# Partition sums of the modulation vectors: one DVE reduction over four transposed tiles in place of four accumulating ACTIVATEs

## The chip, the cores and the metric

The kernel runs on one core of a Trainium2 chip. The time is the device time of one execution in microseconds, taken as the median of several executions. The engines are PE (matrix products, with PEld for its weight loads), ACT (ScalarE), DVE (VectorE), POOL (GpSimd) and SP, whose queue issues most of the DMAs.

## What is computed

Two models run in one launch. The first is two stacked transformer layers over 256 tokens of width 1024. Each layer makes six modulation vectors from a conditioning vector and uses them to shift, scale and gate:

```
mod = jax.nn.silu(c) @ w_ada + b_ada
sh1, sc1, gt1, sh2, sc2, gt2 = jnp.split(mod, 6, axis=-1)
h = adaln(rms_norm(x, g_mix), sh1, sc1)        # h * (1 + scale) + shift
proj = h @ w_in                                # q, k, v and gates of two attentions
x = x + gt1[:, None, :] * (mixed @ w_out)
h = adaln(rms_norm(x, g_mlp), sh2, sc2)
u = jnp.square(jax.nn.relu(h @ w_up))
x = x + gt2[:, None, :] * (u @ w_down)
```

The second model is a layer with a pooling mixer and sixteen experts, then a layer with attention and sixteen experts; both take modulation vectors made in the same way from the same kind of product. Everything is in fp32.

## The kernel before

A vector of 1024 modulation values is a 1 x 1024 by 1024 x 1024 product. `ada_piece` (L335) does it without PE's main stream: the 1024 x 1024 block of the weight matrix comes in eight row pieces of 128 x 1024, and each piece is scaled by its 128 values of silu(c), one to a partition, and added to an accumulator `aacc` of 128 x 1024, by ACT for the first piece (L344) and by DVE for the seven others (L347). When the eighth piece is in (q == 7), the 128 partitions of `aacc` have to be summed. For 24 of the vectors this is done in two halves of four 128 x 128 blocks: PE transposes four blocks (L355) into a PSUM tile `tr`, of which there is one buffer, and four ACTIVATEs with `accum_out` (L358) sum one block each along its free side into a column of `u`. Each such ACTIVATE is followed by an instruction that reads the accumulator out. DVE then adds the bias (L367) and the vector `mod[m, v, j]` is there. The other vectors go through eight products with a vector of ones (L363).

Around this runs the main stream. All weights come as fp32 through SP's queue into seven `raw` buffers. `pump` (L297) splits a piece on chip into a high part `H` (ACT, L303) and a low part `L` (DVE, L304), of which five buffers each exist, and PE multiplies in three passes, high by high (L149), low weights (L150), low activations (L151). Modulation pieces come in the same list between the weight pieces, so `pump` serves both.

The norms ahead of the projections, `norm_1` and `norm_T_`, work on two tiles of 128 tokens: ACT sums squares (L542), POOL makes the reciprocal root, DVE scales the rows (L544), PE transposes them (L558), ACT (L573) and DVE (L571) apply shift and scale to alternate blocks, ACT casts the high part (L575) and DVE subtracts for the low part (L576). `residual_` multiplies a projection by its gate (L898) and adds it to x (L899); the gate's row is made from its `mod` vector by PE (L381) and ACT (L382). `mod_rows` (L986, L990, L991) is the norm of the second model's first layer.

Nothing here is ordered by hand. A tile scheduler takes the program with its dependencies and its priorities and writes one fixed list for each engine; every engine works its list strictly in order and waits on semaphores. `pump` gives modulation pieces a priority below the main stream's (offset -150), norms and residuals one above it (HP).

## Time and profile before

| | us |
|---|---|
| median of 3 runs | 1456.69 (1452.02 to 1458.51) |
| profiled execution | 1451.84 |
| its span | 1450.0 |
| PE busy | 1312.8 |
| DVE busy | 1184.0 |
| ACT busy | 904.9 |
| POOL busy | 192.9 |

The profile is of one execution, 4.85 us below the median of the runs. The modulation vectors that the change touches are summed between 96.8 and 823.0 us of its span. Stretches are named by the us from the start of the span; the first model runs to about 885 us, its second layer from about 435. A timeline row shows one instruction, or several alike in a row, with the idle time of its engine ahead of it and what ended that.

### The profile page before, as it was taken

The page shows a single profiled execution, that of the slowest core. Times are in us where ns is not written, and L with a number is a line of the kernel's source. Part 1 is how long each engine was busy: PE and PEld are TensorE (multiplying, and loading weights), DVE is VectorE, ACT ScalarE, POOL GpSimd, SP SyncE. Part 2 cuts the span into 40 slices and gives each one's busy share as a digit, 9 for nine tenths or more (in the row PEclk, how much of TensorE's full clock was granted, in tenths as well). Part 3 has the DMA queues.
Part 4 walks back from the last instruction along what each step waited for, and adds up shares of the span by engine and source line. Part 5 has one row for each costly group of instructions (what it writes and reads, how often), then busy time and mean ns, then how long its engine had stood idle before and what let it go on. Part 6 is the DMA issues. An engine that isn't in the chain of part 4 may idle for free. (4 is left out here: it accounts for less than half of the span.)

```text
span 1450.0 us, 20231 instructions
## 1 busy us (share of the span) xinstructions
PE 1312.8 (91%) x6943; PEld 1036.2 (71%) x6943; DVE 1184.0 (82%) x1719; ACT 904.9 (62%) x1726; POOL 192.9 (13%) x183
## 2 busy tenths in 40 slices
PE   3889999999998899988999998699998879989897
PEld 2666777898987667767899887577665756766575
DVE  6886697867778988898999888599888798598696
ACT  2476845665656678566765544399784558567584
POOL 0340011000002300121000022322211220110000
PEclk9998998999999999997999999699999999989899
DMA  9676686799784667886888987699986534259781
GB/s 368 199 250 199 231 295 218 274 305 317 266 305 132 217 190 251 267 252 226 298 318 282 338 297 233 204 349 327 324 305 223 165 110 145 89 193 375 290 310 53
DMA packets 109363, 362.16 MB, mean 250 GB/s; under 512 B 17998, under 2 KB 21558, under 8 KB 109248
## 3 DMA queue, kind: packets, MB, share of 16 engines
q1 hardware_dynamic: 105456, 351.26, 70.1%
q0 software_dynamic: 3360, 7.91, 2.3%
q10 hardware_dynamic: 432, 1.57, 0.3%
q8 instruction: 58, 0.95, 0.3%
q14 instruction: 57, 0.47, 0.1%
HBM read 351.70 MB, written 12.88 MB: 251 GB/s over the span
## 5 line engine op out<-in xcount | busy, mean ns | idle before, releaser
L303 ACT CAST H<-raw 128x1024 fp32r<-128x1024 f32 x331 | 345.7, 1049 | 227.3 <-PE acc L151 89.2
L304 DVE TENSOR_TENSOR L<-raw,H 128x1024 fp32r<-128x1024 f32 x331 | 410.0, 1247 | 70.0 <-ACT H L303 67.0
L347 DVE SCALAR_TENSOR_TENSOR page<-raw,sc,page 128x1024 f32<-128x1024 f32 x218 | 279.9, 1293 | 20.5 <-DMA raw<-in_w_ada_dram 11.8
L149 PE MATMUL mm<-H,page 128*128 128x512 f32 (+1 forms) x416 | 168.3, 407 | 15.3 <-ACT page L575 10.5
L150 PE MATMUL mm<-L,page 128*128 128x512 f32 (+1 forms) x416 | 166.1, 400 | 0.1
L151 PE MATMUL mm<-H,page 128*128 128x512 f32 (+1 forms) x416 | 165.4, 399 | 0.9 <-DVE page L576 0.8
L304 DVE TENSOR_TENSOR L<-page,H 128x1024 fp32r<-128x1024 f32 x104 | 125.3, 1222 | 29.5 <-ACT H L303 27.8
L149 PE MATMUL acc<-H,page 128*128 128x512 f32 x352 | 138.5, 394 | 0.0
L151 PE MATMUL acc<-H,page 128*128 128x512 f32 x352 | 138.5, 393 | 0.0
L150 PE MATMUL acc<-L,page 128*128 128x512 f32 x352 | 138.3, 393 | 0.0
L303 ACT CAST H<-page 128x1024 fp32r<-128x1024 f32 x104 | 108.3, 1053 | 40.2 <-PE mm L151 25.2
L800 PE MATMUL mm<-page,H 128*128 128x256 f32 x448 | 127.7, 286 | 0.0
L803 PE MATMUL mm<-page,L 128*128 128x256 f32 x448 | 127.6, 285 | 0.0
L802 PE MATMUL mm<-page,H 128*128 128x256 f32 x448 | 127.3, 284 | 0.0
L149 PE MATMUL mm<-H,gH 128*96 128x512 f32 x256 | 105.7, 413 | 8.9 <-PEq L1231 6.5
L149 PEld LDWEIGHTS mm<-H,page 128*128 128x128 f32 x416 | 81.5, 196 | 36.2 <-ACT page L575 12.9
L151 PE MATMUL mm<-H,gL 128*96 128x512 f32 x256 | 103.9, 406 | 1.3 <-DVE gL L1405 1.3
L150 PE MATMUL mm<-L,gH 128*96 128x512 f32 x256 | 103.0, 402 | 0.0
L151 PEld LDWEIGHTS mm<-H,page 128*128 128x128 f32 x416 | 81.4, 196 | 19.2 <-DVE page L576 3.3
L150 PEld LDWEIGHTS mm<-L,page 128*128 128x128 f32 x416 | 81.8, 197 | 16.2 <-issue 1.7
L800 PEld LDWEIGHTS mm<-page,H 128*128 128x128 f32 x448 | 86.1, 192 | 0.8
L802 PEld LDWEIGHTS mm<-page,H 128*128 128x128 f32 x448 | 85.8, 192 | 0.5
(377 smaller groups left out, 2530.2 us busy)
## 6 DMA issues: line engine op xcount, KB each, us to landing
raw<-in_w_mod_dram SPq DMA_DIRECT2D x94, 512.0 KB, 4.5
raw<-in_w_ada_dram SPq DMA_DIRECT2D x92, 512.0 KB, 5.1
raw<-in_w_in_dram SPq DMA_DIRECT2D x68, 512.0 KB, 4.4
raw<-in_moe_gu_dram SPq DMA_DIRECT2D x64, 512.0 KB, 6.3
raw<-in_w_up_dram SPq DMA_DIRECT2D x61, 512.0 KB, 5.3
raw<-in_w_down_dram SPq DMA_DIRECT2D x61, 512.0 KB, 5.0
page<-in_moe_gu_dram SPq DMA_DIRECT2D x61, 512.0 KB, 8.0
page<-in_moe_wd_dram SPq DMA_DIRECT2D x36, 512.0 KB, 11.0
```

Source lines behind the costliest of these rows:

```text
L149: mm(ps, sH, wH, start=start, stop=False)
L150: mm(ps, sH, wL, start=False, stop=False)
L151: mm(ps, sL, wH, start=False, stop=stop)
L303: s.nc.scalar.copy(H, src)
L304: s.nc.vector.tensor_sub(Lo, src, H.bitcast(F32))
L347: nc.vector.scalar_tensor_tensor(a, raw, c, a, ALU.mult, ALU.add)
L800: nc.tensor.matmul(o, a, H[q // 2][:, 2 * (q % 2) + k], start=q == 0 and k == 0 and f % 2 == 0, stop=False, skip_group_check=True)
L802: nc.tensor.matmul(o, a, Lo[q // 2][:, 2 * (q % 2) + k], start=False, stop=False, skip_group_check=True)
L803: nc.tensor.matmul(o, b, H[q // 2][:, 2 * (q % 2) + k], start=False, stop=q == 3 and k == 1 and f % 2 == 1, skip_group_check=True)
```

## The change

The four ACTIVATEs of a half become one DVE `tensor_reduce`, which sums along the innermost side of the tile seen as 128 x 4 x 128 and writes the four columns of `u` at once. The transposes ahead of it and the addition of the bias behind it stay.

```diff
--- before.py
+++ after.py
@@ -353,9 +353,7 @@
                         t = s.tr()
                         for i in range(4):
                             nc.tensor.transpose(t[:, i * P:(i + 1) * P], s.aacc[v][:, (4 * h + i) * P:(4 * h + i + 1) * P], s.ident)
-                        for i in range(4):
-                            o = t[:, i * P:(i + 1) * P]
-                            nc.scalar.activation(o, o, AF.Copy, accum_out=u[:, 4 * h + i:4 * h + i + 1])
+                        nc.vector.tensor_reduce(u[:, 4 * h:4 * h + 4], t.rearrange("p (a b) -> p a b", b=P), AX.X, ALU.add)
                     t = u
                 else:
                     t = s.mm() if m == 0 and j < 2 else s.tr()
```

192 ACTIVATEs and 192 accumulator reads leave ACT's list, 48 reductions enter DVE's. Since the scheduler places everything by its own reckoning, other instructions move as well. Lines behind 358 have a number lower by 2 in the changed kernel: L558 is L556 there, L576 is L574, L381 is L379.

The second norm of the first layer, on PE: `mm_2069` and `mm_2045` are the end of the out projection, `mm_2235` and `mm_2211` the start of the up projection, and `acc_2179` and `acc_2184` the second tile of tokens. Before:

```order
L151 MATMUL mm_2069<-H_2083,page_1919 128x512
L355 MATMUL tr_2004<-cst,page_1735 128x128 x4
L355 MATMUL tr_2013<-cst,page_1735 128x128 x4
L149 MATMUL mm_2235<-H_2089,page_2159 128x512
L150 MATMUL mm_2235<-L_2090,page_2159 128x512
L151 MATMUL mm_2235<-H_2089,page_2161 128x512
```

After, the same place, where the first group of transposes still stands:

```order
L151 MATMUL mm_2045<-H_2059,page_1901 128x512
L355 MATMUL tr_1986<-cst,page_1717 128x128 x4
L149 MATMUL mm_2211<-H_2065,page_2135 128x512
L150 MATMUL mm_2211<-L_2066,page_2135 128x512
L151 MATMUL mm_2211<-H_2065,page_2137 128x512
```

and further down, around the second group:

```order
L556 MATMUL acc_2179<-cst,page_2172 128x128 x4
L556 MATMUL acc_2184<-cst,page_2172 128x128 x4
L150 MATMUL mm_2211<-L_2217,page_2136 128x512
L151 MATMUL mm_2211<-H_2216,page_2138 128x512
L149 MATMUL mm_2211<-H_2225,page_2136 128x512
L150 MATMUL mm_2211<-L_2226,page_2136 128x512
L151 MATMUL mm_2211<-H_2225,page_2138 128x512
L149 MATMUL mm_2211<-H_2225,page_2136 128x512
L150 MATMUL mm_2211<-L_2226,page_2136 128x512
L151 MATMUL mm_2211<-H_2225,page_2138 128x512
L355 MATMUL tr_1992<-cst,page_1717 128x128 x4
```

The second group of transposes has moved from right behind the first to behind the transposes of the second tile of tokens (L556) and eight more products.

The second norm of the second layer, on DVE, from the scaled rows (L544, now L542) to the low part of the first tile's second half (L576, now L574). Before:

```order
L304 TENSOR_TENSOR L_6253<-raw_6084,H_6252 128x1024
L571 TENSOR_SCALAR q_1375_6189<-acc_6179,acol_6170,mod_3469 128x128
L571 TENSOR_SCALAR q_1376_6196<-acc_6184,acol_6170,mod_3469 128x128
L304 TENSOR_TENSOR L_6263<-raw_6096,H_6262 128x1024
L571 TENSOR_SCALAR q_1375_6189<-acc_6179,acol_6170,mod_3469 128x128
L571 TENSOR_SCALAR q_1376_6196<-acc_6184,acol_6170,mod_3469 128x128
L367 TENSOR_TENSOR mod_6019<-acol_1330_6000,cols 128x8
L347 SCALAR_TENSOR_TENSOR page_6071<-raw_6042,sc,page_6071 128x1024
L576 TENSOR_TENSOR page_6168<-q_1375_6189,page_6166 128x4x128
L347 SCALAR_TENSOR_TENSOR page_6070<-raw_6074,sc,page_6070 128x1024
L576 TENSOR_TENSOR page_6169<-q_1376_6196,page_6167 128x4x128
```

After:

```order
L304 TENSOR_TENSOR L_6139<-raw_5972,H_6138 128x1024
L304 TENSOR_TENSOR L_6145<-raw_5976,H_6144 128x1024
L569 TENSOR_SCALAR q_1375_6081<-acc_6071,acol_6062,mod_3421 128x128
L569 TENSOR_SCALAR q_1376_6088<-acc_6076,acol_6062,mod_3421 128x128
L356 TENSOR_REDUCE acol_1330_5904<-tr_5905 128x4
L569 TENSOR_SCALAR q_1375_6081<-acc_6071,acol_6062,mod_3421 128x128
L347 SCALAR_TENSOR_TENSOR page_5962<-raw_5864,sc,page_5962 128x1024
L574 TENSOR_TENSOR page_6060<-q_1375_6081,page_6058 128x4x128
L569 TENSOR_SCALAR q_1376_6088<-acc_6076,acol_6062,mod_3421 128x128
L304 TENSOR_TENSOR L_6155<-raw_5988,H_6154 128x1024
L574 TENSOR_TENSOR page_6061<-q_1376_6088,page_6059 128x4x128
```

Both L304 now stand ahead of the four blocks to which shift and scale are applied (L569), and the first reduction stands among these. The second one and the bias come right behind this stretch.

The end of the first model, on PE: `acc_61..` (`acc_62..` before) is the last down projection, `mm_8281` and `mm_8287` (`mm_8425` and `mm_8431` before) the row of the gate by which its result is multiplied. Before:

```order
L151 MATMUL acc_6235<-H_8468,page_8098 128x512
L149 MATMUL acc_6235<-H_8468,page_8097 128x512
L1092 MATMUL mm_8329<-Mt_8324,Q_1788_8322 96x32 x4
L381 MATMUL mm_8425<-cst,mod_4078 128x128 x4
L381 MATMUL mm_8431<-cst,mod_4078 128x128 x4
L150 MATMUL acc_6235<-L_8469,page_8097 128x512
L381 MATMUL mm_8440<-cst,acol_8437 128x128 x4
L381 MATMUL mm_8446<-cst,acol_8437 128x128 x4
L381 MATMUL mm_8453<-cst,mod_4630 128x128 x4
L381 MATMUL mm_8459<-cst,mod_4630 128x128 x4
L151 MATMUL acc_6235<-H_8468,page_8098 128x512
```

After:

```order
L151 MATMUL acc_6129<-H_8330,page_7954 128x512
L149 MATMUL acc_6129<-H_8330,page_7953 128x512
L150 MATMUL acc_6129<-L_8331,page_7953 128x512
L151 MATMUL acc_6129<-H_8330,page_7954 128x512
L1090 MATMUL mm_8185<-Mt_8180,Q_1788_8178 96x32 x4
L379 MATMUL mm_8281<-cst,mod_4018 128x128 x4
L379 MATMUL mm_8287<-cst,mod_4018 128x128 x4
L379 MATMUL mm_8296<-cst,acol_8293 128x128 x4
L379 MATMUL mm_8302<-cst,acol_8293 128x128 x4
L379 MATMUL mm_8309<-cst,mod_4564 128x128 x4
L379 MATMUL mm_8315<-cst,mod_4564 128x128 x4
```

The small product L1090 (L1092) and three pairs of L379 (L381), each pair one row spread over 128 partitions, stood among the last down projection's products, 31 of which came behind them; now all of them stand behind the last one.

ACT there, from the last two copies of those rows to the sum of squares of the second tile (L986, now L984). Before:

```order
L382 COPY page_8452<-mm_8453 128x512
L382 COPY page_8452<-mm_8459 128x512
L344 ACTIVATE page_8497<-raw_8404,sc 128x1024
L303 CAST H_8513<-raw_8478 128x1024
L986 ACTIVATE hrow_8583,ss_8584<-x 128x1024
L303 CAST H_11949<-raw_8481 128x1024
L303 CAST H_11961<-raw_8495 128x1024
L303 CAST H_11973<-raw_8499 128x1024
L382 COPY page_8607<-mm_8608 128x512
L382 COPY page_8607<-mm_8614 128x512
L382 COPY page_8620<-mm_8621 128x512
L986 ACTIVATE hrow_8593,ss_8594<-x 128x1024
```

After:

```order
L380 COPY page_8308<-mm_8309 128x512
L380 COPY page_8308<-mm_8315 128x512
L303 CAST H_8369<-raw_8334 128x1024
L984 ACTIVATE hrow_8439,ss_8440<-x 128x1024
L344 ACTIVATE page_8353<-raw_8260,sc 128x1024
L303 CAST H_11805<-raw_8337 128x1024
L984 ACTIVATE hrow_8449,ss_8450<-x 128x1024
```

The two sums of squares have come together: the first stands two instructions behind the copies, the second three further on.

## Rows read from the trace of the kernel before

**Rows 1.** The page, part 1: busy us (share of the span) x instructions of each engine.

```profile
PE 1312.8 (91%) x6943; PEld 1036.2 (71%) x6943; DVE 1184.0 (82%) x1719; ACT 904.9 (62%) x1726; POOL 192.9 (13%) x183
```

**Rows 2.** Everything of line 358; duration ns min/median/max, then who waited for it.

```profile
L358 ACT ACTIVATE tr<-tr x192: 251/262/298, 96.8 to 822.8; 128x128 f32<-128x128 f32 x192
L358 ACT ACTIVATION_READ_ACCUMULATOR tr<-tr x192: 180/194/214, 97.0 to 823.0; 128x1 f32 x192
...
  PE tr L355: 5.7, 6
```

**Rows 3.** DVE grouped by line and form: busy us, mean ns of one, idle before it.

```profile
L1589 DVE TENSOR_REDUCE mx<-acc 128x1 f32<-128x512 f32 x32 | 21.5, 684 | 1.2 <-PE acc L1587 1.0
...
L923 DVE TENSOR_REDUCE mx<-acc 128x1 f32<-128x256 f32 x32 | 13.3, 414 | 0.0
...
L922 DVE TENSOR_REDUCE mx<-acc 128x1 f32<-128x128 f32 x32 | 9.1, 285 | 9.7 <-PE acc L919 9.7
```

**Rows 4.** Waits of PE, 80 to 830 us: us in total, times, longest.

```profile
PE mm L149 <- ACT page L575: 8.1, 5, 2.9
...
PE tr L355 <- ACT tr L358: 5.7, 6, 2.5
```

**Rows 5.** Timeline of PE, 244 to 249: start, us, what [idle before <-releaser].

```profile
247.14 0.66 PE L355 MATMUL tr<-cst,page 128*128 128x128 f32 x4 [2.45 <-ACT tr L358]
...
248.72 0.58 PE L151 MATMUL mm<-H,page 128*128 128x512 f32 x1
```

**Rows 6.** Timeline of DVE, same stretch.

```profile
246.77 1.22 DVE L304 TENSOR_TENSOR L<-raw,H 128x1024 fp32r<-128x1024 f32 x1
247.98 0.69 DVE L576 TENSOR_TENSOR page<-q,page 128x512 fp32r<-128x512 f32 x1
```

**Rows 7.** Timeline of PE, first and second norm of the second layer, 450 to 657.

```profile
450.93 1.10 PE L558 MATMUL acc<-cst,page 128*128 128x128 f32 x8 [0.73 <-DVE page L544]
...
652.79 1.12 PE L355 MATMUL tr<-cst,page 128*128 128x128 f32 x4 [0.83 <-ACT tr L358]
655.85 1.12 PE L355 MATMUL tr<-cst,page 128*128 128x128 f32 x4 [1.94 <-ACT tr L358]
```

**Rows 8.** Timeline of DVE, second layer: attention, second norm, up projection.

```profile
515.87 0.42 DVE L964 TENSOR_TENSOR page<-acc,page 128x256 fp32r<-128x256 f32 x1 [1.57 <-ACT page L963]
...
657.11 0.69 DVE L576 TENSOR_TENSOR page<-q,page 128x512 fp32r<-128x512 f32 x1
...
721.32 1.22 DVE L304 TENSOR_TENSOR L<-raw,H 128x1024 fp32r<-128x1024 f32 x1
```

**Rows 9.** Windows: length, busy PE, PEld, DVE, ACT, POOL, then PEclk, DMA share, GB/s.

```profile
640.00:660.00 20.00, 14.48 (x61) 11.09 (x60) 18.98 (x23) 13.02 (x39) 2.71 (x3) 0.79 0.88 263
...
680.00:800.00 120.00, 119.32 (x778) 107.96 (x777) 114.59 (x118) 75.10 (x144) 3.15 (x2) 1.00 0.86 297
```

**Rows 10.** Timeline of PE: first use of what DVE made at 721.32.

```profile
729.65 0.28 PE L803 MATMUL mm<-page,L 128*128 128x256 f32 x1
```

**Rows 11.** Timeline of PE, end of the last down projection, 871 to 892.

```profile
871.70 1.07 PE L381 MATMUL mm<-cst,mod 128*128 128x128 f32 x8
...
881.41 0.39 PE L151 MATMUL acc<-H,page 128*128 128x512 f32 x1
...
891.62 0.59 PE L1028 MATMUL acc<-band,hrow 128*128 128x136 f32 x1 [4.56 <-DVE hrow L991]
```

**Rows 12.** Timeline of DVE, 872 to 909.

```profile
872.98 0.69 DVE L898 TENSOR_TENSOR q<-acc,page 128x512 f32<-128x512 f32 x1 [0.69 <-ACT page L382]
...
887.49 3.48 DVE L990 SCALAR_TENSOR_TENSOR hrow<-x,rstd,page 128x512 f32<-128x512 f32 x2 [0.74 <-POOL rstd L156]
...
907.63 1.41 DVE L990 SCALAR_TENSOR_TENSOR hrow<-x,rstd,page 128x512 f32<-128x512 f32 x2
```

**Rows 13.** Timeline of ACT, 872 to 886.

```profile
872.36 3.16 ACT L382 COPY page<-mm 128x512 f32<-128x512 f32 x6 [3.77 <-PE mm L381]
...
884.31 1.07 ACT L986 ACTIVATE hrow<-x 128x1024 f32<-128x1024 f32 x1
```

## The prediction

> **What bounds the kernel now.** I read the busy times first: PE is at work for 91% of the span, DVE for 82%, ACT for 62% [rows 1]. So the question for every edit is whether PE waits less or more, and the next engine to fear is DVE, not ACT. Then I read the changed line by itself: 192 ACTIVATEs of 262 ns and as many accumulator reads of 194 ns, and six waits of PE for them, 5.7 us in all [rows 2]. Then the list of PE's waits while modulation vectors are summed: those 5.7 us, of which one is 2.5 us, and 8.1 us for the cast of a norm's high part (L575), which is on ACT too and stands there in one list with L358 [rows 4]. Last I read the timelines of the places with these waits, and of the places where the new lists differ. There the reader is to see what stands next in line behind each wait, since that decides whether anything is gained.
>
> **The cost of the operation.** ACT loses 192 x (262 + 194) ns = 87.6 us [rows 2]. That hides behind PE nearly everywhere and by itself is worth nothing; what is worth something is the time of ACT instructions queued behind it at the norms. DVE gains 48 reductions of 128 x 512 out of PSUM to 128 x 4. The trace has none of that form. The nearest row is the reduction of 128 x 512 in PSUM to 128 x 1, 684 ns; the lower bound is the one of 128 x 256, 414 ns; the upper bound is four of 128 x 128, 4 x 285 ns = 1.14 us [rows 3]. I take 684 ns, because the number of elements read is the same: 48 x 0.684 = 32.8 us (19.9 to 54.7) on DVE. The transposes cost PE what they did.
>
> **First layer, second norm (241 to 257 us).** PE's longest wait for L358, 2.45 us, ends at 247.14 [rows 5]. The second group of transposes is now elsewhere, so this wait is gone. What is late next is on DVE: the third product of the stream needs the low part of the norm (L576), which starts at 247.98 because a split (L304, 1.22 us from 246.77) is ahead of it [rows 6]. That product started at 248.72 [rows 5] and can start no sooner than the 248.67 at which L576 ends, bar 0.2 us if DVE gets its blocks from ACT a little sooner. The transposes (0.66 us) fall further down, where PE waits for the second tile anyway. I take -0.5 us; the ends are 0 and the whole wait, -2.45.
>
> **Second layer, first norm (436 to 455).** ACT's sum of squares of the second tile no longer has two L358s right ahead of it, so the wait of 0.73 us before L558 at 450.93 [rows 7] should go: 0.456 us each for two is 0.9. I take -0.7; the ends are 0 and -0.9.
>
> **Second layer, second norm (642 to 669).** Two waits for L358, 0.83 and 1.94 us, stand before the transposes at 652.79 and 655.85 [rows 7]. Now one group is gone from here, but the first reduction stands on DVE behind both splits and two blocks, some 2.5 us of work, so that PE's second group waits until about 655, in one wait and not two. Behind it the low part, at 657.11 before [rows 8], can come about 0.6 us sooner. The group that left adds its 0.66 us of transposes later, where the second tile's cast is waited for. Net -0.3; the ends are the whole of both waits, -2.8, and +0.7 if the moved group is not hidden.
>
> **Second layer, attention (495 to 540).** Four reductions enter DVE's list between the softmax's small reductions and the splits. They are 4 x 0.68 = 2.7 us, and DVE stood idle for 1.57 us there [rows 8], which leaves 1.1. I take +1.0; the ends are 0 and +2.5.
>
> **First layer's attention and both out projections.** Eight reductions now stand ahead of the small sums that PE waits for with POOL. If none were hidden they would cost 5.5 us; POOL's part of the wait hides most. I take +0.5, from -0.6 (an ACT instruction comes sooner) to +2.
>
> **The other reductions** lie in long stretches of weight products. From 680 to 800 us PE is busy 119.32 of 120 us, so nothing can be gained; DVE is busy 114.59 of 120, so there is 5.4 us of room for eight reductions, 5.5 us [rows 9]. DVE is also well ahead: the split that ends at 722.5 [rows 8] is first used at 729.65 [rows 10], 7.1 us later. I take 0, from 0 to +5.
>
> **End of the first model (870 to 895).** This is a side effect: three pairs of row-making products move behind the last down projection product. Each pair took 1.07 us [rows 11], so the last product, before at 881.41 [rows 11], ends some 3.2 us sooner, at about 878.6. But one of these rows is the gate without which no residual can be made: before, DVE's L898 followed ACT's copy already at 872.98 [rows 12], and the six copies were done at 875.5 [rows 13]. Now the pairs end at 878.6 + 3.2 = 881.8 and the sixth copy (3.16 / 6 = 0.53 us) at 882.3. Behind it ACT has a cast, the first tile's sum of squares, a first modulation piece, another cast and then the second tile's sum. These are all 1024 wide, like the sum itself with 1.07 us [rows 13]: 882.3 + 4 x 1.07 = 886.6, against 884.31 before, 2.3 us late. What follows is a chain of single steps, reciprocal root, L990, L991, and PE idle for 4.56 us until 891.62 [rows 11]. One thing may give back: two L990 took 3.48 us beside POOL's L1048 and 1.41 us elsewhere [rows 12], 2.1 us of contention for each of the two pairs, and POOL's own work moves too. So the ends are 2.3 - 4.2 = -1.9 and +3.3 (with PE's pairs not all hidden); I take +2.0, near the side without relief, because POOL's two additions still follow the second reciprocal root.
>
> **The sum** is -0.5 - 0.7 - 0.3 + 1.0 + 0.5 + 0 + 2.0 = +2.0 us. On the profiled execution that is 1451.84 + 2.0 = 1453.8. That execution lies 4.85 us under the median of the runs, so by the median the time is 1456.69 + 2.0 = 1458.7. A measurement of this kernel can tell about 0.5%, 7.3 us, from no change: I forecast no change that can be told.
>
> **Rival, faster: the norms were bound by ACT after all.** Then PE gets back all 5.7 us of its waits for L358 and, with four L358s out of the way of a cast (4 x 0.456 = 1.8 us), 1.3 of the 8.1 us waited for L575. The granted clock helps as well: in 640 to 660 us, with stalls in it, it was 0.79 on average, between the levels 1.2 and 2.4 GHz; PE's 14.48 busy us there [rows 9] at 1.00 would be 14.48 x 0.21 = 3.0 us less. If the end of the first model costs nothing, the sum is -5.7 - 1.3 - 3.0 + 1.5 = -8.5: 1448.2. For it speaks that PE's waits name ACT; against it, that DVE's split ahead of L576 ends within 0.1 us of the same time [rows 6].
>
> **Rival, slower: DVE loses its lead.** DVE works its list in order. A reduction that it reaches before PE has made the transposes holds up every split behind it, and the one `tr` buffer holds up PE's next group until DVE has read it. Place: 680 to 800 us. With 1.14 us each and 1 us of waiting each, eight reductions take 17.1 us; less 5.4 of room and 7.1 of lead, PE loses 4.6. The stretches around 570 and 810 us have four reductions each and could lose as much again together, say 8 us in all. With the +2.0 that is 1466.7. It decides when waiting and work together exceed room and lead, 12.5 us for eight; by the price I take they are 5.5 plus waits of about half the groups, some 4 us, and the lead holds. The Trainium skill, Perfetto Trace Analysis, section Optimizing Scalar/DVE Operations, speaks for this rival: where DVE is saturated, work that either engine can do is better given to Scalar, and this change does the reverse. The trace agrees with its condition: DVE 114.59 and ACT 75.10 of 120 us.
>
> **How the numbers follow.** Forecast, within 0.5%: 0.60, with its own range 1452 to 1464 (the terms' ends taken half each way). Faster rival 0.16, slower rival 0.24: against the first speaks a row, against the second only an estimate of waits. The range from 1449 to 1467 reaches both rivals' times and leaves out what lies beyond them, about 0.15. Faster by over 0.5% means under 1449.4, slower means over 1464.0; the chances are those of the rivals.
>
> **What would show it.** The new line should be 48 reductions of about 0.68 us. PE's wait for `tr` at 244.7 should be gone, with a wait for L574 (L576 before) in its place at about 248.5; at 655 one wait for the DVE reduction. Between 680 and 800 PE should stay over 119 busy us; if it waits for L304 there, the slower rival is right. The second tile's sum of squares should start about 5 us after the first model's last copy of rows, and PE's stall before L1026 (L1028 before) end about 2 us later than the rest of the program is shifted; if it ends earlier, the term that I priced highest has the wrong sign. If PE goes straight from the first transposes into products at full clock at the norms, the faster rival holds and the forecast is wrong.

## The result: slower by 0.8%

| | before | after |
|---|---|---|
| median of nine runs, us | 1451.89 | 1465.47 (1453.15 to 1469.29) |
| ratio to before | | 1.0081, interval 1.0061 to 1.0101 |
| profiled execution, us | 1451.84 | 1468.82 |

The medians are 13.6 us apart; the ratio makes it 11.8. One of before's nine runs took 2567 us; the median hardly feels it, and the ratio leaves it out. The time lies in the stated range, at its upper end, and it is nearer to the slower rival's (1466.7) than to the forecast's (1458.7). That is in part luck. The forecast was built on 1456.69, the median of before's first three runs, and all nine give 1451.89. From that base the same sums make 1453.9 for the forecast and 1461.9 for the slower rival, 2.0 and 10.0 us up, so the step that was measured is larger than either. The profile of after is of a run 3.4 us above its median.

Busy times of after, from its page (answer to [rows 1]):

```profile
PE 1318.0 (90%) x6943; PEld 1040.9 (71%) x6943; DVE 1205.8 (82%) x1767; ACT 848.5 (58%) x1342; POOL 192.6 (13%) x183
```

ACT lost 56.4 us of work (904.9 before; 87.6 were priced), DVE gained 21.8 (1184.0; 32.8 were priced) and PE is busy 5.2 us longer (1312.8) with the same products. The new line by itself, with what DVE waited for ahead of it and who waited for it:

```profile
L356 DVE TENSOR_REDUCE acol<-tr x48: 659/686/693, 95.3 to 815.5; 128x4 f32<-128x512 f32 x48
...
  PE tr L355: 5.1, 8
...
  PE tr L355: 8.1, 7
```

Each reduction took 0.686 us, as priced. PE waits for it 8.1 us, where it waited 5.7 for the four ACTIVATEs [rows 2, 4].

**Where the time went.** PE has the same products in both traces, so the start of one product in after, less its start in before, tells how far ahead or behind the changed kernel is. It is 2.4 us ahead at 84 us (times of before), 9.1 at 262, 4.5 at 549, 6.8 at 700 and 2.0 at 828; it is 4.4 behind at 843, 13.5 at 932 and 16.9 at 1412. From 960 on the distance wanders by some 3 us. So the change first gains, and loses more between 700 and 932, in two places.

Not all of this is waiting. The products from 84 to 262 took 177.7 us before and 171.0 after (a window of each, columns as in [rows 9]):

```profile
84.20:261.90 177.70, 163.82 (x774) 123.50 (x773) 134.11 (x208) 115.59 (x276) 23.02 (x17) 0.94 0.68 229
81.80:252.80 171.00, 159.29 (x774) 119.94 (x773) 136.99 (x216) 105.51 (x213) 20.32 (x18) 0.98 0.70 234
```

PE stood idle 2.2 us less, and it was busy 4.5 us less with the same 774 products, at a granted clock of 0.98 and not 0.94 on average. Before, the clock stood at 0.50, the lower of its two levels (1.2 and not 2.4 GHz), from 109.1 to 119.3, from 214.9 to 221.7 and from 249.0 to 252.4; after, from 104.1 to 107.5 and from 240.7 to 244.1.

**The gain** begins at one place that I had not looked at closely, the softmax of the first layer's attention. Before, ACT waits for DVE's reciprocal of the denominators, and PE for ACT:

```profile
109.84 1.49 ACT L941 ACTIVATE sm<-sm,den 128x128 f32<-128x128 f32 x4 [3.25 <-DVE den L938]
...
110.29 0.48 PE L947 MATMUL acc<-cst,sm 128*128 128x128 f32 x1 [5.33 <-ACT sm L941]
```

After, on DVE, ACT and PE:

```profile
103.87 0.15 DVE L935 TENSOR_TENSOR den<-den,es 128x4 f32<-128x4 f32 x1
104.28 0.16 DVE L936 RECIPROCAL den<-den 128x4 f32<-128x4 f32 x1
...
104.53 1.50 ACT L939 ACTIVATE sm<-sm,den 128x128 f32<-128x128 f32 x4 [1.50 <-DVE den L936]
...
104.00 0.70 PE L150 MATMUL mm<-L,page 128*128 128x512 f32 x1 [2.02 <-DVE L L304]
...
105.35 0.41 PE L945 MATMUL acc<-cst,sm 128*128 128x128 f32 x1
```

The scheduler put DVE's small sums in another order. The sum and reciprocal of the denominators now start at 103.87, ACT's L939 (L941 before) starts at 104.53 and not at 109.84, and PE's wait of 5.33 us is gone. One of 2.02 us has come ahead of it, for a split. The 5.33 us are also where before's stretch of 10.2 us at half clock begins; after has 3.4 us of it there. From 84 to 130 PE's idle time falls by only 1.1 us (5.9 to 4.8) and its time for these products by some 4.5, so most of what is gained here comes through the clock behind the wait. No run holds the new order with the old sums, so how much of the gain is the order and how much the work taken off ACT stays open.

**The norms.** The waits changed as predicted. At the first layer's second norm PE no longer waits for `tr`; what it waits for instead is the cast and the low part:

```profile
238.59 0.50 PE L149 MATMUL mm<-H,page 128*128 128x512 f32 x1 [2.32 <-ACT page L573]
...
239.99 0.50 PE L151 MATMUL mm<-H,page 128*128 128x512 f32 x1 [0.67 <-DVE page L574]
...
248.98 0.50 PE L149 MATMUL mm<-H,page 128*128 128x512 f32 x1 [0.76 <-ACT page L573]
```

At the second layer's there is one wait for the reduction in place of the two in [rows 7], behind a wait for the scaled rows (2.72 us before):

```profile
649.52 1.97 PE L556 MATMUL acc<-cst,page 128*128 128x128 f32 x8 [4.76 <-DVE page L542]
653.17 1.09 PE L355 MATMUL tr<-cst,page 128*128 128x128 f32 x4 [1.69 <-DVE acol L356]
```

**First loss, 690 to 840.** Window of after, columns as in [rows 9]:

```profile
690.00:840.00 150.00, 139.03 (x907) 125.38 (x906) 137.35 (x145) 70.42 (x85) 9.72 (x4) 0.98 0.84 285
```

and of before:

```profile
690.00:840.00 150.00, 149.06 (x978) 134.51 (x976) 136.14 (x139) 94.19 (x196) 6.47 (x4) 1.00 0.88 310
```

PE lost 10.0 us of work, although ACT had 23.8 us less to do; DVE was as busy as before. PE's waits there (us in total, times, longest) in before come to this:

```profile
PE tr L355 <- ACT tr L358: 0.3, 2, 0.2
```

and in after to this:

```profile
PE tr L355 <- DVE acol L356: 4.1, 4, 1.5
PE mm L801 <- DVE L L304: 4.1, 2, 2.6
PE mm L798 <- ACT H L303: 2.3, 1, 2.3
```

Together 10.5 us (two waits of 0.3 us are left out): four waits for the reduction, and three for a split's part that DVE or ACT had not made in time. In the part of this stretch that the prediction looked at, 680 to 800, PE's busy time fell from 119.32 to 115.83 us, and there the waits are for the reduction:

```profile
PE tr L355 <- DVE acol L356: 3.1, 3, 1.5
```

DVE stood idle ahead of none of the twelve reductions between 690 and 840. So PE's transposes were there when DVE came to them; the reductions came late because splits and modulation pieces stand between them on DVE's list, and the next group of transposes needs the one `tr` buffer. The split's waits are the sign of a lost lead: before, DVE's L304 ended 7.1 us ahead of its use [rows 8, 10]; after, there is a place at 800.63 where PE stands for it. This and the last two of these waits in PE's timeline:

```profile
800.63 0.39 PE L801 MATMUL mm<-page,L 128*128 128x256 f32 x1 [1.46 <-DVE L L304]
...
834.86 0.58 PE L798 MATMUL mm<-page,H 128*128 128x256 f32 x1 [2.30 <-ACT H L303]
...
838.27 0.58 PE L801 MATMUL mm<-page,L 128*128 128x256 f32 x1 [2.61 <-DVE L L304]
```

The last two waits have a second cause ahead of them. ACT's timeline shows casts that waited for weights, this one and one at 833.76 with 4.75 us:

```profile
826.67 1.05 ACT L303 CAST H<-raw 128x1024 fp32r<-128x1024 f32 x1 [6.12 <-DMA raw<-in_w_up_dram]
```

and SP's queue shows why the weights were late. L392 and L393 are the way of one modulation row out to memory and back, spread over all partitions; L393 has to wait for L392, and all loads behind it on the queue wait too, from 821.73 to 825.54:

```profile
820.58 0.29 SPq L392 DMA_DIRECT2D rowd<-rowc  x1
...
821.36 0.37 SPq L293 DMA_DIRECT2D raw<-in_w_mod_dram  x1
825.54 0.33 SPq L393 DMA_DIRECT2D row<-rowd  x1
```

**Second loss, 840 to 932.** Here the lists of the engines have another order. The context path is what the second model does with its context tokens (norm, pooling mixer, routing); the program works it in small steps into the first model's last up and down projection, and its last steps, the routing, begin with the small product L1216. Before, 43 products of the last down projection stood behind L1216; after, 6. So the context path, the gate's row and the second model's rows now all come when the down projection is as good as over. PE:

```profile
884.32 0.18 PE L1214 MATMUL tr<-M,less 128*128 128x16 f16 x1
...
896.86 1.24 PE L1026 MATMUL acc<-band,hrow 128*128 128x136 f32 x4 [4.25 <-DVE hrow L989]
...
907.18 6.61 PE L1033 MATMUL acc<-page,page 128*128 128x256 f32 x16 [3.25 <-issue]
```

L1216 (L1214) is at 884.32 (868.35 before), the rows are made from 886.53 on, and ACT copies them and sums squares:

```profile
887.20 3.04 ACT L380 COPY page<-mm 128x512 f32<-128x512 f32 x6 [5.43 <-PE mm L379]
...
894.03 1.10 ACT L984 ACTIVATE hrow<-x 128x1024 f32<-128x1024 f32 x1
```

(Between the two rows are a cast, the first tile's sum and a modulation piece.) The second tile's sum starts 3.8 us behind the last of the six copies (890.24 to 894.03). PE's stall ends at 896.86, 5.24 us later than in [rows 11]; 4.4 us of this were there at 843. Then more is lost behind it. POOL's two additions (887.42 to 889.76 and 891.04 to 893.78) were beside L990 and L991 before [rows 12], and DVE went straight on to L1020, which scales the weights that PE's L1035 takes:

```profile
890.89 3.44 DVE L991 TENSOR_TENSOR hrow<-hrow,page 128x512 f32<-128x512 f32 x2
894.25 1.28 DVE L1020 TENSOR_TENSOR page<-page,page 128x512 f32<-128x512 f32 x2
```

After, POOL's additions start later, and meet two other instructions (timelines of POOL and DVE):

```profile
899.66 5.73 POOL L1046 TENSOR_TENSOR x<-x,page 128x1024 f32<-128x1024 f32 x2 [3.09 <-ACT page L380]
```

```profile
894.75 1.41 DVE L988 SCALAR_TENSOR_TENSOR hrow<-x,rstd,page 128x512 f32<-128x512 f32 x2 [0.76 <-POOL rstd L156]
...
897.28 1.41 DVE L988 SCALAR_TENSOR_TENSOR hrow<-x,rstd,page 128x512 f32<-128x512 f32 x2
...
899.81 3.38 DVE L347 SCALAR_TENSOR_TENSOR page<-raw,sc,page 128x1024 f32<-128x1024 f32 x1
...
903.23 3.25 DVE L347 SCALAR_TENSOR_TENSOR page<-raw,sc,page 128x1024 f32<-128x1024 f32 x1
906.40 1.28 DVE L1018 TENSOR_TENSOR page<-page,page 128x512 f32<-128x512 f32 x2
```

L988 (L990) is at its short time, 1.41 us. But two modulation pieces, L347, now stand between the norm and L1018 (L1020), and beside POOL they take 3.38 and 3.25 us where one takes 1.32 us on average. PE starts L1033 (L1035) at 907.18, where it started it at 895.03. The trace puts its last 3.25 us of waiting to no engine; L1018's first half ends at about 907.0, right ahead of it. The row that L1018 needs was there by 899.66, since POOL's addition takes the one made behind it. The contention that I hoped to be rid of had only moved, to work in front of the same chain.

These waits are the smaller part of the second loss. The same 482 products in a window of before, the same in one of after (each window cuts one or two more), and a piece of the latter:

```profile
840.00:940.00 100.00, 80.73 (x484) 69.97 (x484) 74.29 (x159) 39.86 (x65) 26.57 (x26) 0.85 0.70 237
```

```profile
845.20:954.50 109.30, 87.92 (x483) 75.68 (x484) 76.35 (x164) 42.30 (x68) 26.65 (x25) 0.81 0.69 237
872.10:878.90 6.80, 6.80 (x21) 5.64 (x21) 5.09 (x23) 0.25 (x2) 2.54 (x2) 0.50 1.00 352
```

They take 9.3 us longer, but PE's idle time grows by 2.1 us only (19.3 to 21.4); 7.2 us are PE being busy longer, at a lower granted clock. From 872.1 to 878.9 PE works through the last down projection at 0.50 without a wait, and starts a product every 0.43 us and not every 0.23; before, none of that projection behind 843 ran so. The sixteen L1033 at 907.18 took 6.61 us, nearly all at 0.50 (906.3 to 913.1); the next sixteen took 3.70.

### The profile page after: what moved, and what is told of

The parts are those of the page before. It is cut to its first block, busy times and chain, and to the rows that moved or that the text cites. A ratio compares the mean times of both kernels' runs of the same rounds, so it can differ in the third digit from the quotient of the medians.

```text
span 1467.0 us, 19830 instructions
## 1 busy us (share of the span) xinstructions
PE 1318.0 (90%) x6943; PEld 1040.9 (71%) x6943; DVE 1205.8 (82%) x1767; ACT 848.5 (58%) x1342; POOL 192.6 (13%) x183
## 5 line engine op out<-in xcount | busy, mean ns | idle before, releaser
L304 DVE TENSOR_TENSOR L<-raw,H 128x1024 fp32r<-128x1024 f32 x331 | 406.7, 1237 | 74.2 <-ACT H L303 69.9
L347 DVE SCALAR_TENSOR_TENSOR page<-raw,sc,page 128x1024 f32<-128x1024 f32 x218 | 285.2, 1320 | 14.0 <-DMA raw<-in_w_ada_dram 11.8
L149 PE MATMUL mm<-H,page 128*128 128x512 f32 (+1 forms) x416 | 165.8, 401 | 15.5 <-ACT page L573 10.2
L151 PE MATMUL mm<-H,page 128*128 128x512 f32 (+1 forms) x416 | 164.4, 397 | 1.8 <-DVE page L574 1.8
L304 DVE TENSOR_TENSOR L<-page,H 128x1024 fp32r<-128x1024 f32 x104 | 125.0, 1221 | 30.5 <-ACT H L303 27.8
L801 PEld LDWEIGHTS mm<-page,L 128*128 128x128 f32 x448 | 86.5, 193 | 4.6 <-DVE L L304 4.6
L798 PEld LDWEIGHTS mm<-page,H 128*128 128x128 f32 x448 | 86.6, 193 | 3.1 <-ACT H L303 2.5
```

Source lines behind the costliest of these rows:

```text
L149: mm(ps, sH, wH, start=start, stop=False)
L151: mm(ps, sL, wH, start=False, stop=stop)
L304: s.nc.vector.tensor_sub(Lo, src, H.bitcast(F32))
L347: nc.vector.scalar_tensor_tensor(a, raw, c, a, ALU.mult, ALU.add)
L798: nc.tensor.matmul(o, a, H[q // 2][:, 2 * (q % 2) + k], start=q == 0 and k == 0 and f % 2 == 0, stop=False, skip_group_check=True)
L801: nc.tensor.matmul(o, b, H[q // 2][:, 2 * (q % 2) + k], start=False, stop=q == 3 and k == 1 and f % 2 == 1, skip_group_check=True)
```

## Experiments

All make the sums by one line, in which C says which modulation vectors are reduced on DVE; `m` is the model and layer (0 and 1 the first model's layers, 2 and 3 the second's):

```
-                        for i in range(4):
-                            o = t[:, i * P:(i + 1) * P]
-                            nc.scalar.activation(o, o, AF.Copy, accum_out=u[:, 4 * h + i:4 * h + i + 1])
+                        if C: nc.vector.tensor_reduce(u[:, 4 * h:4 * h + 4], t.rearrange("p (a b) -> p a b", b=P), AX.X, ALU.add)
+                        for o, i in [(t[:, i * P:(i + 1) * P], 4 * h + i) for i in range(0 if C else 4)]:
+                            nc.scalar.activation(o, o, AF.Copy, accum_out=u[:, i:i + 1])
```

Line numbers are those of before. Differences in us are between medians; each is against the runs of before on the same chip (1451.5 to 1452.2).

### Which reductions cost: C by layer

**Early ones alone** (`C = m < 2`, 20 of 48, all before 450 us).

> Reductions only for the vectors of the first model (20 of the 48 halves, all before 450 us); the 28 others keep their four ACTIVATEs. Theory A (the gain is early, the loss is late, from DVE's lost lead and from the order at the end of the first model): faster than the kernel before by 5 to 9 us, 1443 to 1447 us, with PE as far ahead at 450 us as in the changed kernel (8 us) and the end of the first model as before. Theory B (each reduction costs DVE time wherever it stands): slower by some 20/48 of 12 us, about 1457 us.

Measured: 1445.42, ratio 0.9952 (0.992 to 0.9984), 6.5 us faster than before. Its runs were granted a clock of 0.957 to 0.965 (median 0.962), those of before beside them 0.952 to 0.963 (0.957): this gain too goes with a higher clock. **Late ones alone** (`C = m >= 2`, 28, from some 500 us).

> Reductions only for the vectors of the second model (28 halves, from 500 us on); the 20 earlier ones keep their ACTIVATEs. Theory A: all of the loss and none of the gain, so slower than the changed kernel itself, 1468 to 1474 us, level with the kernel before at 480 us. Theory B: 28/48 of 12 us, about 1459 us.

Measured: 1473.65, ratio 1.0157 (1.0112 to 1.0202), 21.7 us slower. **The last four** (`C = m == 3`, at 805 to 815).

> Reductions only for the last vectors (four halves, at 805 to 815 us); all others keep their ACTIVATEs, and the order at the end of the first model is that of the kernel before. If what starves the split at 820 to 840 us is the work of these four themselves, PE stalls there and the time is 5 us longer; if it is a lead lost earlier, between 700 and 800 us, no stall there and no change, within 2 us of before.

Measured: 1450.30, ratio 0.9979 (0.9955 to 1.0003), no difference that can be told.

What follows: the change is a gain and a loss, -6.5 + 21.7 = 15.2 against 13.6 for the whole. The four reductions just ahead of the waits at 834 don't make these by themselves. With the early ones alone PE loses nothing from 690 to 840 (window, columns as above):

```profile
690.00:840.00 150.00, 148.70 (x979) 134.13 (x978) 132.33 (x137) 91.61 (x193) 8.45 (x4) 1.00 0.88 301
```

This kernel is the fastest that leaves nothing out. It beats before by 0.2 to 0.8% and after by about 1.3%.

### The late waits and the second loss: the gate, the queue, a buffer, or the order?

**The gate's row sooner.** The changed kernel, with the row of the gate made ahead of the last up projection's products:

```
+            if i == 7: s.flush_ada(l, 5); gt = s.row(s.mod[l, 0, 5])
             u2 = up(i)
...
-        s.flush_ada(l, 5)
-        gt = s.row(s.mod[l, 0, 5])
```

> The changed kernel with one more edit: the row of the gate of the last down projection is made ahead of the last up projection and no longer behind the last product. If the wait of the residual for that row is what the end of the first model costs, the first pooling product (L1028) comes 3 to 6 us sooner and the time is 1459 to 1462 us; if the loss there comes from the routing path, which stays late, or lies ahead of 840 us, no change, 1465 us.

Measured: 1469.83, ratio 1.0109 (1.0069 to 1.0149), no better than after. The theory that the residuals wait for the gate gets no support, but the run doesn't rule it out, because more than the row has moved. The scheduler set the context path still later, now behind all of the down projection, and PE waits for that path instead (timeline of PE; the wait is the one in the bracket):

```profile
893.50 0.17 PE L1216 MATMUL tr<-M,less 128*128 128x16 f16 x1 [5.51 <-DVE M L1075]
```

**The modulation rows off SP's queue.** The changed kernel, with both DMAs of `far_row` issued by POOL:

```
-        nc.sync.dma_start(d, u)
-        nc.sync.dma_start(r, d.rearrange("a b -> (a b)").partition_broadcast(P))
+        nc.gpsimd.dma_start(d, u)
+        nc.gpsimd.dma_start(r, d.rearrange("a b -> (a b)").partition_broadcast(P))
```

> The changed kernel with the two small DMAs of a context row (L392 out to DRAM, L393 back) issued from POOL's queue and not from SP's, in which L393 waits for L392's landing ahead of the weight pieces. Theory Q (late DVE frees raw buffers late, and then a row's round trip in SP's queue holds back the next pieces): the waits of ACT for weight pieces of 6.1 and 4.8 us at 820 and 829 us go, and with them PE's waits of 2.3 and 2.6 us at 832 and 836; 1456 to 1461 us. Theory D (DVE alone is late): PE still waits there for L304, 1465 us. The context path moves a little ahead in the order as well (24 and not 6 of the last down projection's products stand behind L1216).

Measured: 1465.50, ratio 1.0099 (1.0062 to 1.0136). The waits of 2.30 and 2.61 us at 834 to 838 are gone, but for 0.55, so the queue did make the weights late there. The total didn't move; two new waits stand in PE's timeline:

```profile
805.45 0.47 PE L355 MATMUL tr<-cst,page 128*128 128x128 f32 x1 [4.83 <-DVE page L347]
...
847.21 0.27 PE L390 MATMUL tr<-cst,acol 128*8 128x128 f32 x1 [4.52 <-DVE mod L367]
```

The same edit on the kernel with early reductions alone:

> Reductions for the first model's vectors only, and the row trips in POOL's queue: the two edits that help by theory A and Q together. If the row trips cost something even without late pieces, 1440 to 1444 us; if not, as with the first edit alone, 1445 us.

Measured: 1451.00, ratio 0.9991 (0.9965 to 1.0017): it doesn't help there either, and by the medians gives back most of what that kernel had gained. Neither expectation (up to 1445) allowed for that, and it wasn't followed.

**One page more for weights** in the second layer's up and down projections of the changed kernel (`EXTRA = (2, 9, 0, 1, 7, 8, 1, 1)`, last entry 0 before):

> The changed kernel with one more page lent to the weight pieces during the second layer's MLP (the last entry of EXTRA, 0 before, is 1), so that one more piece can be on its way; the order at the end of the first model stays that of the changed kernel. By theory Q one more piece of 512 KB covers about 2 us of the two waits at 820 to 840 us: 1460 to 1463 us. By theory D no change, 1465 us.

Measured: 1465.05, ratio 1.0077 (1.0037 to 1.0117). The two waits at 834 and 837 are still there, 1.99 and 2.69 us. A page more doesn't help.

**The order alone.** All sums on ACT, as in before; the gate's row is made behind the last up projection's products (`u2 = up(i)`, then the added line above). With this the scheduler puts the context path as late as in after: 7 products stand behind L1216. The lists of PE and DVE are those of before up to 837 us, bar a few places at 416 to 428; behind 837 they are neither those of before nor those of after.

> All 48 halves with their four ACTIVATEs, as before, but the gate's row of the last down projection made at the last up projection, which lets the scheduler put the context path and the other rows behind the last product, nearly as in the changed kernel (7 products behind L1216, 43 in the kernel before). If this order alone costs the 9 us that the changed kernel loses between 845 and 930 us, 1458 to 1463 us; if that loss comes from being late there, no change from before, 1450 to 1454 us.

Measured: 1464.17, ratio 1.0077 (1.0048 to 1.0106), 12.6 us slower without a single reduction on DVE. PE is 0.5 us ahead of before at 843 and 11.1 behind at 932. It shows two things that after shows as well, two pieces of work on DVE (this time splits, 1.22 us elsewhere) that stand ahead of L1020 and run beside POOL's additions, and a wait of PE behind them. Timelines of DVE, POOL and PE:

```profile
898.67 5.60 DVE L304 TENSOR_TENSOR L<-raw,H 128x1024 fp32r<-128x1024 f32 x2
...
897.56 5.62 POOL L1048 TENSOR_TENSOR x<-x,page 128x1024 f32<-128x1024 f32 x2 [6.32 <-ACT page L382]
...
905.48 0.77 PE L1035 MATMUL acc<-page,page 128*128 128x256 f32 x1 [6.95 <-DVE page L1020]
```

So a late place of the context path by itself costs about as much as after loses between 843 and 932 (9.1 us). It isn't lost in the same way: for the products from 840 to 940 PE's idle time grows by 8.6 us here, in after by 2.1. That the late place is what costs after its 9.1 us is likely, and not shown.

### The first loss with the end held nearly in one order

A context path that comes *sooner* than in before could be a cure. `CTXP` says at which of the up projection's eight steps it goes on; in each of three kernels its last five entries are moved from (7, 0) to (6, 1), which puts 48 products behind L1216 in all three. From 820 us on the second and third have the same lists but for the sums; those of the first still differ from theirs in places:

```
-CTXP = [(4, 0), (5, 1), (6, 0), (7, 0), (7, 0), (7, 0), (7, 0), (7, 0)]
+CTXP = [(4, 0), (5, 1), (6, 0), (6, 1), (6, 1), (6, 1), (6, 1), (6, 1)]
```

With the changed kernel:

> The changed kernel with the steps of the context path written one up projection sooner (the five entries (7, 0) of CTXP are (6, 1)), so that its small products, L1216 and the gate's rows stand 43 and more products ahead of the last one, as in the kernel before or sooner; up to there the lists are those of the changed kernel. Theory E (the order at the end of the first model costs 11 us, by the run of the old sums in that order): 1453 to 1456 us, level with before. Theory L (the splits' lost lead, PE's waits at 690 to 840 us, costs most of it): those waits stay and the time with them, 1460 to 1465 us.

Measured: 1466.91, ratio 1.0093 (1.0057 to 1.0129), above both. With before:

> The kernel before with that same edit of CTXP and all ACTIVATEs. A control: if the sooner context path is worth something by itself, 1446 to 1450 us; if not, as before, 1452 us.

Measured: 1462.33, ratio 1.0073 (1.0049 to 1.0098). It costs before 10.6 us, which neither expectation had: sooner is as bad as later. PE then waits in the down projection for splits, 1.18 us at 847.83 and 2.36 at 850.92.

With early reductions alone:

> Reductions for the first model's 20 halves only, and that same edit of CTXP. By the gain of the early reductions alone (6.5 us), 6 us under the control, 1440 to 1446 us. Against the run with all 48 it gives what the 28 late reductions cost when the order at the end is held: by theory L 8 to 10 us, by theory E alone 0 to 2.

Measured: 1454.38, ratio 1.0008 (0.9990 to 1.0026).

What follows: with the path at one place, the early reductions give 1454.38 - 1462.33 = -8.0 us (with one order at the end), and the 28 late ones cost 1466.91 - 1454.38 = 12.5 (with nearly one order there).

### Is it DVE's time?

The changed kernel, with each reduction reading 16 of every 128 columns. The transposes, the one `tr` buffer and ACT's freedom stay, but a reduction takes a third of the time. The order does not stay, since the scheduler knows the shorter time: between 500 and 840 us PE's list differs from that of after in some 97 places and DVE's in some 130.

```
-                        nc.vector.tensor_reduce(u[:, 4 * h:4 * h + 4], t.rearrange("p (a b) -> p a b", b=P), AX.X, ALU.add)
+                        nc.vector.tensor_reduce(u[:, 4 * h:4 * h + 4], t.rearrange("p (a b) -> p a b", b=P)[:, :, 0:16], AX.X, ALU.add)
```

> All 48 reductions in their places, but each sums only 16 of the 128 columns of a block (it leaves out seven eighths of the sum), so that it takes about 0.2 us and not 0.68. If the work of the reductions on DVE is what eats the lead, PE's waits for L356 and L304 between 690 and 840 us go from about 11 us to under 3, and PE is at 825 us where the kernel with the early reductions alone is (some 4 us ahead of before); if it is DVE's waiting in line for the transposes, they stay. The scheduler sees the shorter instruction and places the context path between the two known orders (29 products behind L1216), so the whole time is between 1447 and 1460 us by either.

Measured: 1444.68, ratio 0.9942 (0.9924 to 0.9960). The reductions, PE's waits for them and the window from 690 to 840:

```profile
L356 DVE TENSOR_REDUCE acol<-tr x48: 196/219/226, 95.0 to 803.0; 128x4 f32<-128x64 f32 x48
```

```profile
PE tr L355 <- DVE acol L356: 3.5, 3, 2.3
```

```profile
690.00:840.00 150.00, 146.53 (x972) 133.46 (x972) 137.62 (x155) 76.22 (x97) 15.02 (x4) 1.00 0.87 305
```

28 late reductions are 28 x (0.686 - 0.219) = 13.1 us shorter, and PE has 7.5 us more of work done in the stretch than in after. The result is not quite either theory's: PE's waits from 690 to 840 fall to 3.5 us and not below 3, PE is 12.2 us ahead at 828 where 4 were expected, and the whole time lies below the range. The waits for a split, 6.4 us in after, are gone; those for the reduction itself are nearly what they were (3.5 against 4.1) although it takes a third of the time. So it speaks for DVE's time as what costs the splits their lead, and against it as what PE's waits for the reduction depend on; these go by the reduction's place in DVE's list. Since the lists differ everywhere, time and order aren't told apart by this run, neither here nor at the end (29 products behind L1216).

### The runs beside each other

How far PE is behind before (minus: ahead) at the same products, us, worked out from the timelines:

| at, us | after | early only | late only | last four | order alone | short sums |
|---|---|---|---|---|---|---|
| 84 | -2.4 | -2.1 | -0.8 | -2.2 | -1.3 | -2.7 |
| 262 | -9.1 | -10.1 | -3.1 | -4.3 | -0.9 | -7.2 |
| 549 | -4.5 | -3.2 | -4.0 | -0.5 | -0.6 | -6.9 |
| 700 | -6.8 | -4.9 | -2.7 | -2.3 | -0.8 | -13.7 |
| 828 | -2.0 | -4.5 | 2.6 | -1.1 | -0.5 | -12.2 |
| 843 | 4.4 | -5.3 | 8.1 | -1.9 | -0.5 | -12.9 |
| 932 | 13.5 | -0.7 | 17.7 | -2.2 | 11.1 | -8.6 |
| 1412 | 16.9 | -0.6 | 21.2 | 0.7 | 16.2 | -8.5 |

Single executions: "late only", "last four" and "order alone" have nothing changed before 400 us, and stand at -0.9 to -4.3 at 262. So some 4 us of any number here are chance, and it goes with the granted clock: for the products from 84 to 262 it was 0.94 on average before, 0.94 for "order alone", 0.96 for "late only" and "last four", and 0.98 for after and "early only", the two of these with early reductions. Read with that, the columns agree. Kernels with early reductions gain at once; those with the 28 late ones in full length lose 10.8 to 11.2 from 700 to 843; those with the late context path lose 9.1 to 11.6 from 843 to 932; "last four" loses nowhere. One column is a warning: "early only" has before's lists from 820 on and still loses 4.6 us from 843 to 932. There PE ran at 0.50 from 858.3 to 865.1, busy all the time, which before did not. In round numbers, after is -7 (gain, -6.5 and -8.0 by medians) + 12 (late reductions) + 9 (between 843 and 932, order and clock) = +14; measured were 13.6 by medians and 11.8 by the ratio.

**What stays open.** How the two losses share what after lost is known only to some 5 us: the late reductions cost 12.5 us with the path held and 9.1 as "late only" less "order alone" (21.7 - 12.6), and the "early only" column shows 4.6 us of the second loss with no change of order. Every edit moved lists and granted clock along with the work, and no run holds either. That the longer time on DVE is what moves the scheduler's order at the end is not shown by a run; the late place of the path goes with late reductions (6 products behind L1216 with all and with the late ones alone, 43 with the early ones alone or the last four), and that is all. After's runs spread by 16 us, more than those of the kernel with short sums (4.5), and the spread goes with the clock: the fastest, 1453.15 us, was granted 0.964 on average, the slowest, 1469.29 us, 0.955. Why one execution is granted more than another isn't shown.

## Why the prediction was right or wrong, point by point

- **Cost of the reduction** (0.684 us): right, 0.686. The choice of the row with the same number of elements read was the right one. What ACT gives up was priced too high: 87.6 us as the sum of all durations, 56.4 by ACT's busy time. In part that is overlap: the first accumulator read starts at 97.00, and its ACTIVATE ends at 97.08.
- **Norms** (-0.5, -0.7, -0.3): the mechanisms were right; the wait for `tr` at 247 gave way to 2.32, 0.67 and 0.76 us for the cast and the low part, and at 653 there is one wait for the reduction. That the sums of these three places came out as priced can't be told within the 4 us of chance. The faster rival, by which PE gets all its waits for L358 back, is wrong at these places: the next wait takes over. (What the prediction set against it was read wrongly: in [rows 5, 6] it is L576 that ends, at 248.67, within 0.1 us of the product that needs it, and the split ahead of it ends at 247.99.) That rival's other half, the clock, was right in kind and at another place, ahead of 262.
- **First layer's attention** (+0.5, -0.6 to +2): this step failed, with the wrong sign. I priced the added work and no change of order. What changed was ACT's 3.25 us of waiting for a reciprocal that stood late on DVE's list, which the row at 109.84 showed, and the half clock behind it. Most of the early gain of 6.5 to 8.0 us starts there: at 119 after is 8.0 us ahead, at 84 it was 2.4.
- **Second layer's attention** (+1.0, 0 to +2.5): can't be told. After loses 4.1 us from 495 to 540, but "early only" and "last four" lose 5.0 and 4.0 there without a single reduction in it, and "late only", with them, loses 0.7.
- **The other reductions** (0, 0 to +5): the step that failed most, 10.8 to 12.5 us. Two errors. I looked at the eight reductions between 680 and 800 and set 5.4 us of room and 7.1 of lead against them, but 28 reductions stand behind 500 us, 19.2 us of DVE time, and a lead is spent once, not once in each stretch. And I took the lead from one place (7.1 us ahead at 729.65), and not from the place where it was shortest. No row shows how short that lead is elsewhere; PE's first wait for a split came at 800.63. The slower rival had the right place and half of the mechanism. PE's 119.32 busy us between 680 and 800 fell to 115.83, and what PE waited for there was the one `tr` buffer, 3.1 us, as it says; a wait for L304 came only behind 800. The other half did not come: DVE waited for the transposes of none of these reductions, and with 5.5 us of work in place of 17.1 of work and waits the rival's own condition, 12.5, was not met. Its time came near by other sums. More than half of the loss (6.4 us of the 11.2 between 700 and 843) falls between 828 and 843, where ACT waits for late weights as well, which it didn't name. The page of the Trainium skill that I set beside this rival, Perfetto Trace Analysis, section Optimizing Scalar/DVE Operations, says that giving Scalar some of the work may make sense where DVE is saturated. The runs with late reductions agree, at 12.5 us, and those with early ones don't, at -6.5 and -8.0.
- **End of the first model** (+2.0, -1.9 to +3.3): the chain was described rightly as far as PE's stall. The second tile's sum came 3.8 us behind the last copy (4.3 by the working, "about 5" among its signs), L990 took 1.41 and not 3.48 us, and the stall ended 5.2 us later, 0.8 more than PE was behind at 843. Behind it the step failed: I counted POOL's contention as a possible refund of 4.2 us and didn't ask what DVE would do while POOL was at work. It met two L347 ahead of L1020, PE waited 3.25 us, and with the half clock, which I had priced for the norms alone, the loss grew to 13.5 by 932. A late path costs 12.6 us by its own run, where I had +2.0.
- **The sum.** The forecast of no change was wrong on two terms, each 7 to 12 us too low, and one, the attention's, some 6 us too high. The time is inside the range only because the range reached to the slower rival and stood on a base that three runs had put 4.8 us too high: the measured step of 13.6 us (11.8 by the ratio) is more than the 10.3 by which the range went beyond that base.

## What to carry to other kernels

Where one engine feeds the bound engine through all of a long stretch, I would now take the room for new work on it as its lead at the shortest place plus its idle time, spent once for the whole stretch, and add up all the new work against it; the runs fit this and don't prove it. Look also at what stands between two instructions that share one buffer. Move work between engines by place and not by kind: here the same substitution gained 6.5 us where DVE waits in short chains and lost 12.5 where DVE keeps the splits ahead. Where a scheduler orders the program again, follow each changed chain to its next wait and one beyond, since a reordered end cost as much without the change as with it. And split a gain or a loss into idle time and busy time: where PE does the same products in another time, the granted clock has changed, and a list of waits doesn't show it.

## What I had not expected of the hardware

Beside POOL's L1048, four kinds of DVE instruction took longer than elsewhere: two L990 of 128 x 512 took 3.48 us [rows 12] and 1.41 without it; L347 of 128 x 1024 took 3.38 and 3.25 us against a mean of 1.32; two L304 took 5.60 against 1.22 each, and two L991 took 3.44 against 1.28. The loss is 1.9 to 3.2 us for each row, so what POOL's 5.7 us cost goes by what stands on DVE's list meanwhile, and by whether PE waits for it.

The granted clock stood at 0.50 also where PE had not just waited: from 872.1 to 878.9 in after and from 858.3 to 865.1 with early reductions alone it was busy for 6.80 of 6.80 us, and the waits nearest before, 2.61 and 2.50 us, had ended some 34 and 15 us earlier. Which activity decides that isn't shown by these runs.
